# A backbone block on one core: a new order of the jobs of its first part, and five tiles of the second modulation's columns summed by TensorE instead of two

## The chip, the cores and the metric

The kernel is written in Tile for one NeuronCore of a Trainium2 chip. TensorE (PE in the profile), VectorE (DVE), ScalarE (ACT), GpSimd (POOL) and SyncE (SP, which only issues transfers here) each run their own instructions in order and wait for one another by semaphores. The metric is the device time of one execution in microseconds (us); lower is better. Three timed runs of the kernel before are given, and one profiled execution with its trace.

## The reference, cut to what matters

The block has one layer: a pooling mixer, a residual with layer norm, a SwiGLU feed-forward and a second residual with layer norm, over 1024 tokens of width 1024. A conditioning vector `c` gives six modulation vectors.

```python
mod_x = silu(c) @ mod_w + mod_b                   # (1024) @ (1024, 6144)
sh1, sc1, g1, sh2, sc2, g2 = split(mod_x, 6)
hx = x * (1.0 + sc1) + sh1
# window means (2, 4, 8, 16 tokens; one per 256 columns) less the row itself, then a 256x256 product per group
ox = multiscale_pool(hx, pool_w, pool_scale)
x = layer_norm(ALPHA * x + g1 * ox, ln_g[0], ln_b[0])
h = x * (1.0 + sc2) + sh2
gt, up = split(h @ ffn_w_in, 2)                   # 1024 -> 2 x 2816
x = layer_norm(ALPHA * x + g2 * ((silu(gt) * up) @ ffn_w_out), ln_g[1], ln_b[1])
```

All of it is in float32; the large products are made of three products of rounded parts (hi*hi, hi*lo, lo*hi), for which each operand is first split in two.

## The kernel before

It has three parts. The **first part** (to 227 us) computes everything up to the normalised rows and starts the feed-forward's gate products; the **loop** over 22 blocks of 128 hidden columns (to about 480 us) does the feed-forward's first product by a Strassen-like scheme; the **last part** does its second product, the residual and the last norm.

The first part is not written in the order in which it runs. Each step is a function, and `job` (L278) files it under its name and a running number, as mod_add.16. `carry_out` (L284) then calls the jobs in the order of the list `ORDER_OF_ISSUE` (L43). Each engine runs the instructions of its own jobs in just that order, so the list sets five queues at once. Which of the 45 large SBUF buffers, 8 PSUM banks and small rows a tile lies in is also a list, `PLACE_OF` (L111): a line is one place, its names are the tiles that use it one after another, and a tile waits until the one before it has been read.

The rows of x are worked on in two halves of four tiles of 128 tokens, `ORDER[0]` (rows 1 to 4) and `ORDER[1]` (5, 6, 7, 0). The jobs:

- mod_load (SP, L369) loads one 128x1024 tile of mod_w, 512 KB. Eight tiles make one modulation vector: mod_load.0 to .7 are SC1, .8 to .15 G1, .16 to .23 SC2, .24 to .31 SH2, .32 to .39 SH1.
- mod_add (DVE, L493, L491) adds a tile times its column of silu(c) into an accumulator. mod_col (PE, L513, L506) then sums the accumulator over the partitions into a column layout: eight matmuls of 128x128 by 128x64, 16 records in the trace. mod_whole (PE, L509, L506) does both for one tile straight from mod_w: again eight such matmuls, added up in the bank. `mod_columns(j, by_tensor)` (L523) makes mod_whole for the tiles in `by_tensor` and mod_add for the others. I call one mod_col or mod_whole a column pass. Before, SC2 had no tile by TensorE and SH2 had tiles 0 and 1 (`BY_TENSOR`, L35).
- pool_inner, pool_outer (PE, L457, L463) make the window means of 128 columns of a half in a bank, pool_hi (ACT) and pool_lo (DVE, L473) split them. Numbers 0 to 7 of pool_outer, pool_hi and pool_lo are the first half, 8 to 15 the second; pool_inner has four for each.
- scale_bank, g1_bank (PE) spread pool_scale and G1 over the partitions, make_g1 multiplies them, pool_w_weigh, pool_w_hi and pool_w_lo fold them and 1+SC1 into pool_w.
- pooled (PE, L587) is 12 matmuls for one row tile and one half of the columns: .0 to .7 are the first half's rows, .8 to .15 the second's. residual (DVE, L604) adds the row, mean, spread, factor and norm make the layer norm, keep_row stores it.
- mod_col_done, finish_gain and finish_shift (DVE) turn the column sums into per-partition factors. turned (PE, L691) transposes 128 columns of four rows, scaled_h (ACT) applies gain and shift, hidden_hi and hidden_lo split.
- gate_load, gate_hi, gate_lo prepare a pair's gate weights; gate_step (PE, L754) is six matmuls of 512 columns; there are 88. gate_first and gate_done (ACT) empty the banks, gate_out stores. Each step needs only the first half's rows.
- SH1's columns (mod_col.3), shift_through, shift_bank, shift_row and bend (among gate steps) correct two rows of the second half; turned.8 to .15 come after these rows' norms. difference, t_hi and t_lo make the loop's operands of them. weights_load, all_sums (POOL, L959), one_hi, two_hi, one_lo, two_lo prepare the loop's weights; `period` (L1233) is one turn of the loop.

The order of the loads on SP holds the stream of transfers: SC1 and rows, G1, pool_w, second rows, SC2, SH2, then gate weights.

Of the kernel before, what the change touches and what calls it, by code (L numbers as in the profile page):

```python
# [48 lines left out]
mod_load.11 mod_add.4 mod_load.12 mod_load.13 mod_load.14 pool_inner.11 pool_inner.3 mod_load.15 pool_inner.15
pool_inner.7 load_pool_w.0 load_pool_w.1 mod_add.5 load_x.4 pool_outer.2 load_x.5 pool_outer.0 pool_hi.2 pool_outer.3  # L50
pool_outer.1 load_x.6 pool_hi.0 pool_inner.24 pool_lo.2 pool_inner.16 load_x.7 pool_inner.25 pool_hi.3 pool_inner.17
mod_load.16 mod_add.6 pool_inner.28 pool_hi.1 pool_inner.20 mod_load.17 pool_inner.26 pool_inner.18 pool_inner.29
mod_load.18 pool_lo.0 pool_inner.21 start_band.0 scale_bank.0 mod_add.7 mod_load.19 end_band.0 scale_bank.1
scale_row.0 mod_add.8 mod_load.20 mod_col.0 scale_row.1 mod_add.9 mod_load.21 pool_inner.27 pool_outer.6
mod_col_done.0 pool_lo.3 pool_inner.19 pool_outer.4 pool_hi.6 pool_inner.30 mod_add.10 mod_load.22 pool_hi.4
pool_inner.22 pool_inner.31 pool_outer.7 pool_inner.23 pool_outer.5 pool_hi.7 mod_add.11 mod_load.23 pool_hi.5
mod_add.12 mod_load.24 mod_add.13 mod_load.25 mod_add.14 mod_load.26 mod_add.15 mod_load.27 g1_bank.0 pool_lo.1
pool_lo.6 pool_lo.4 g1_bank.1 pool_lo.7 pool_lo.5 make_g1.0 make_g1.1 pool_inner.40 pool_inner.32 pool_w_weigh.0
pool_inner.44 pool_w_weigh.1 pool_inner.36 pool_inner.41 pool_w_weigh.2 pool_inner.33 pool_w_weigh.3 pool_inner.56
pool_inner.48 pool_w_weigh.4 pool_inner.45 pool_w_hi.0 pool_inner.37 pool_w_weigh.5 pool_inner.42 pool_w_weigh.6  # L60
pool_inner.34 pool_inner.57 pool_w_lo.0 pool_inner.49 pool_inner.46 pool_inner.38 pool_inner.43 pool_outer.10 pooled.0
pool_w_weigh.7 pool_hi.10 mod_add.16 mod_load.28 pool_w_hi.1 pooled.2 residual.0 mod_add.17 mod_load.29 pooled.4
mod_add.18 mod_load.30 pool_inner.35 pool_outer.8 pool_inner.47 pool_hi.8 pool_outer.11 residual.2 pool_inner.39
pool_outer.9 pool_hi.11 pool_inner.59 mod_add.19 mod_load.31 gate_load.0 gate_load.1 gate_load.2 gate_load.3
gate_load.4 gate_load.5 pooled.6 pool_hi.9 mod_add.20 pool_outer.14 pool_inner.51 pool_outer.12 pool_inner.58
mod_add.21 pool_inner.50 pool_hi.14 pool_hi.12 residual.4 residual.6 pool_inner.60 mod_add.22 pool_inner.61
pool_inner.52 pool_inner.53 mod_add.23 pool_inner.63 pool_outer.15 pool_inner.55 pool_w_lo.1 pool_outer.13
pool_inner.62 pool_inner.54 pool_lo.10 pool_hi.15 mod_add.24 pool_hi.13 mod_whole.0 pool_lo.8 mod_add.25 mod_whole.1
mod_add.26 pooled.1 mod_add.27 residual.1 pooled.3 mod_add.28 mod_add.29 residual.3 mod_col.2 gate_hi.0 mean.0
spread.0 mean.1 gate_lo.0 pooled.5 spread.1 pool_lo.11 pooled.7 factor.0 residual.5 factor.1 norm.0 mod_col.1 mean.2  # L70
residual.7 keep_row.0 spread.2 mean.3 pool_lo.9 spread.3 pool_lo.14 pooled.12 factor.2 finish_gain.0 finish_shift.0
pooled.14 factor.3 norm.1 pool_lo.12 keep_row.1 norm.2 pool_lo.15 pooled.8 norm.3 pool_lo.13 keep_row.2 pooled.13
residual.12 keep_row.3 gate_hi.2 residual.14 turned.0 gate_hi.1 turned.1 residual.13 gate_lo.2 turned.2 scaled_h.0
turned.3 turned.4 scaled_h.1 gate_lo.1 turned.5 hidden_hi.0 turned.6 turned.7 pooled.15 residual.8 scaled_h.2
scaled_h.3 hidden_lo.0 hidden_hi.1 pooled.10 residual.15 scaled_h.4 hidden_lo.1 gate_step.0 scaled_h.5 hidden_hi.2
gate_step.1 residual.10 scaled_h.6 hidden_lo.2 scaled_h.7 gate_step.2 hidden_hi.3 gate_step.3 gate_hi.4 hidden_lo.3
gate_hi.3 gate_step.4 gate_lo.4 gate_hi.5 gate_lo.3 gate_step.5 gate_lo.5 gate_step.6 mod_load.32 gate_first.0
gate_step.7 mod_load.36 mod_add.30 gate_out.0 gate_first.1 gate_step.8 mod_load.33 gate_out.1 gate_step.9 mod_load.34
gate_step.10 mod_load.35 gate_step.11 gate_load.6 gate_load.7 gate_step.12 mod_add.31 gate_done.0 gate_out.2
gate_step.13 gate_step.14 mod_add.32 gate_step.15 load_pool_w.2 load_pool_w.3 mod_add.33 gate_first.2 gate_step.16  # L80
mod_load.37 mod_add.34 gate_out.3 gate_hi.6 gate_step.17 mod_load.38 gate_lo.6 gate_hi.7 gate_step.18 mod_load.39
gate_lo.7 gate_step.19 gate_load.8 gate_load.9 gate_step.20 gate_done.1 gate_out.4 gate_step.21 gate_step.22
mod_add.35 gate_step.23 gate_first.3 gate_step.24 gate_out.5 gate_step.25 mod_add.36 gate_step.26 mod_add.37
gate_step.27 gate_load.10 gate_load.11 gate_hi.8 gate_lo.8 mod_col.3 gate_done.2 gate_out.6 gate_hi.9 gate_step.28
mod_col_done.1 shift_through.0 gate_step.29 gate_lo.9 gate_step.30 shift_through.1 gate_hi.10 gate_step.31 gate_lo.10
gate_first.4 gate_step.32 gate_out.7 gate_hi.11 gate_step.33 gate_lo.11 gate_step.34 gate_step.35 gate_load.12
gate_load.13 gate_step.36 gate_done.3 gate_out.8 gate_hi.12 gate_step.37 gate_lo.12 gate_step.38 gate_hi.13
gate_step.39 gate_lo.13 gate_first.5 gate_step.40 gate_out.9 gate_step.41 gate_step.42 gate_step.43 gate_load.14
gate_load.15 gate_step.44 gate_done.4 gate_out.10 gate_hi.14 gate_step.45 gate_lo.14 gate_step.46 gate_hi.15
gate_step.47 weights_load.0 gate_lo.15 gate_first.6 gate_step.48 gate_out.11 gate_step.49 gate_step.50 gate_step.51  # L90
gate_load.16 gate_load.17 all_sums.0 gate_step.52 gate_done.5 gate_out.12 gate_step.53 one_hi.0 one_lo.0 gate_hi.16
gate_step.54 gate_lo.16 gate_step.55 two_hi.0 gate_first.7 shift_bank.0 two_lo.0 gate_out.13 gate_hi.17 gate_step.56
shift_row.0 gate_lo.17 shift_bank.1 pooled.9 bend.0 bend.2 pooled.11 residual.9 gate_step.57 residual.11 gate_step.58
shift_row.1 bend.1 bend.3 gate_step.59 gate_load.18 gate_load.19 gate_hi.18 gate_hi.19 gate_lo.18 gate_step.60
gate_done.6 gate_lo.19 gate_out.14 gate_step.61 mean.6 spread.6 gate_step.62 mean.7 mean.4 mean.5 spread.7 factor.6
gate_step.63 p1_load.0 weights_load.1 gate_first.8 gate_step.64 factor.7 gate_out.15 spread.4 gate_step.65 spread.5
gate_step.66 factor.4 gate_step.67 gate_load.20 gate_load.21 factor.5 norm.6 keep_row.6 norm.7 gate_step.68 keep_row.7
norm.4 gate_step.69 keep_row.4 norm.5 gate_step.70 keep_row.5 gate_done.7 gate_step.71 gate_out.16 gate_hi.20
gate_lo.20 gate_first.9 gate_step.72 gate_out.17 gate_hi.21 gate_step.73 gate_lo.21 gate_step.74 turned.8 turned.10
scaled_h.8 gate_step.75 scaled_h.10 gate_done.8 turned.12 turned.14 gate_out.18 scaled_h.12 turned.9 scaled_h.14  # L100
turned.11 turned.13 scaled_h.9 turned.15 scaled_h.11 difference.0 gate_step.76 scaled_h.13 scaled_h.15 difference.4
gate_step.77 hidden_hi.4 difference.1 gate_step.78 hidden_hi.5 difference.5 t_hi.0 gate_step.79 gate_first.10 t_lo.0
# [1302 lines left out]
```

## Time and profile before

| what | value |
|---|---|
| time of the three runs, median (lowest to highest) | 761.9 us (760.66 to 762.62) |
| the profiled execution's own time | 765.08 us |
| its span, first to last instruction | 763.3 us |
| mean granted TensorE clock | 0.962 |
| busy share of the span: PE, DVE, ACT, POOL | 96%, 73%, 36%, 22% |
| first gate product, first product of the loop (starts) | 97.7 us, 227.4 us |

A busy share is an average over parts with different limits, so the stretches are to be read one by one. The granted clock is a share of TensorE's full clock; it is 1.00 (2.4 GHz) or 0.50 (1.2 GHz) at any moment. Matmuls overlap, so that the time from one start to the next is shorter than the duration of one. The share of DMA is that of the core's 16 transfer engines.

### The profile page before, as it was taken

Reading aid. Unit: us, or ns where it says so; the run is one execution under the profiler, and the core shown is the slowest. Engines: PE = TensorE matmul, PEld = TensorE weight load, DVE = VectorE, ACT = ScalarE, POOL = GpSimd, SP = SyncE. Lnnn points to the kernel's source line nnn. Section 1 sums busy time; section 2 is a strip of 40 time slices with the busy share of each in tenths; the row PEclk is TensorE's granted clock in tenths of the full one; section 3 lists DMA queues with packets and bytes.
Section 4 is the critical chain, followed back from the end, with each engine's and each line's share of the span. In section 5 each row is a group of like instructions: output and inputs, shape, how many; then the busy total and the mean of one; then the engine's idle time right before and its main releaser. Section 6 shows DMA issues by size and latency. Waiting matters only on the chain.

```text
span 763.3 us, 9102 instructions
## 1 busy us (share of the span) xinstructions
PE 730.3 (96%) x3326; PEld 605.9 (79%) x3326; DVE 559.9 (73%) x675; ACT 275.0 (36%) x353; POOL 165.6 (22%) x126
## 2 busy tenths in 40 slices
PE   6988999999999999999999999999879999999995
PEld 5767988888887888888888888888558888888784
DVE  3598855517198797988889979865369689747985
ACT  0212873435982312213122131123247634344311
POOL 0000000020207554734736447421000000000000
PEclk7578999999999999999999999999999999999998
DMA  8998249685838689999998999699999975764412
GB/s 297 344 409 301 112 148 378 219 247 165 304 113 285 209 276 298 265 278 250 282 297 287 295 202 259 214 288 275 303 365 389 340 234 191 232 229 152 164 58 83
DMA packets 117731, 191.51 MB, mean 251 GB/s; under 512 B 7627, under 2 KB 66707, under 8 KB 117174
## 3 DMA queue, kind: packets, MB, share of 16 engines
...
HBM read 150.79 MB, written 66.06 MB: 284 GB/s over the span
## 4 chain that ended last, share of the span: by engine, by line
PE 65%; issue 16%; DMA 11%; DVE 5%; ACT 2%; POOL 0%; SPq 0%; POOLq 0%; DVEq 0%; ACTq 0%
PE ps_v L895 33%; PE ps_gate L761 13%; PE ps_x L1103 7%; DMA yraw<-in_ffn_w_out 4%; PE ps_y L1103 4%; DMA line_lb<-in_ln_b 3%; PE ps_col L506 2%; DVE acc L491 2%; PE ps_pt L461 1%; DMA a11d<-a 1%; PE ps_ox L262 1%; PE ps_ox L264 1%; PE ps_ox L263 1%; DMA x<-in_x 1%; DVE t L270 1%
## 5 line engine op out<-in xcount | busy, mean ns | idle before, releaser
L270 DVE TENSOR_TENSOR ylo<-yraw,yhi 128x1024 fp32r<-128x1024 f32 x77 | 91.8, 1221 | 34.4 <-ACT yhi L267 23.6
L267 ACT CAST yhi<-yraw 128x1024 fp32r<-128x1024 f32 x77 | 80.0, 1052 | 94.4 <-PE ps_x L1103 31.7
L895 PE MATMUL ps_v<-t,w0h 128*128 128x512 f32 x352 | 109.2, 392 | 0.0
L761 PE MATMUL ps_gate<-h,wih 128*128 128x512 f32 x352 | 109.0, 391 | 0.0
L962 POOL TENSOR_TENSOR s<-raw,raw 128x512 f32<-128x512 f32 x22 | 33.1, 1504 | 320.4 <-DMA raw<-in_ffn_w_in 312.0
L918 ACT ACTIVATE a<-a 128x512 f32<-128x512 f32 x22 | 13.9, 632 | 230.0 <-DVE a L917 230.0
L895 PEld LDWEIGHTS ps_v<-t,w0h 128*128 128x128 f32 x352 | 66.1, 188 | 14.5 <-issue 1.0
L761 PEld LDWEIGHTS ps_gate<-h,wih 128*128 128x128 f32 x352 | 65.7, 188 | 13.8 <-issue 0.5
L1103 PE MATMUL ps_x<-yhi 128*128 128x512 f32 x176 | 69.6, 395 | 5.1 <-ACT u L1310 2.7
L1103 PE MATMUL ps_x<-ylo,yhi 128*128 128x512 f32 x176 | 69.8, 397 | 3.3 <-DVE ylo L270 3.3
L491 DVE SCALAR_TENSOR_TENSOR acc<-mw,s_col,acc 128x1024 f32<-128x1024 f32 x42 | 54.9, 1307 | 23.1 <-DMA mw<-in_mod_w 22.5
L895 PE MATMUL ps_v<-t,w0l 128*128 128x512 f32 x176 | 68.6, 390 | 1.5 <-DVE w0l L270 1.5
L1103 PE MATMUL ps_x<-yhi,ylo 128*128 128x512 f32 x176 | 69.2, 393 | 0.0
L761 PE MATMUL ps_gate<-h,wil 128*128 128x512 f32 x176 | 68.5, 389 | 0.0
L895 PE MATMUL ps_v<-t,ws 128*128 128x512 f32 x264 | 63.4, 389 | 0.0
L895 PEld LDWEIGHTS ps_v<-t,ws 128*128 128x128 f32 x264 | 49.5, 188 | 10.3
L895 PE MATMUL ps_v<-t,w1h 128*128 128x512 f32 x176 | 54.1, 389 | 0.0
L895 PE MATMUL ps_v<-h,w1h 128*128 128x512 f32 x176 | 54.1, 389 | 0.0
L1103 PE MATMUL ps_y<-yhi 128*128 128x512 f32 x132 | 51.4, 390 | 0.9 <-DVE yv L1348 0.9
L1103 PE MATMUL ps_y<-ylo,yhi 128*128 128x512 f32 x132 | 51.4, 389 | 0.0
L1103 PE MATMUL ps_y<-yhi,ylo 128*128 128x512 f32 x132 | 51.3, 389 | 0.0
L1125 POOL TENSOR_TENSOR yrow<-yrow,line_lg 128x224 f32<-128x224 f32 x1 | 0.9, 913 | 229.3 <-ACT yrow L1185 229.3
...
## 6 DMA issues: line engine op xcount, KB each, us to landing
...
```

The lines of the kernel that those rows point to most:

```text
L262: nc.tensor.matmul(ps, lh, rh, start=first, stop=False)
L263: nc.tensor.matmul(ps, lh, rl, start=False, stop=False)
L264: nc.tensor.matmul(ps, ll, rh, start=False, stop=last)
L267: nc.scalar.copy(hi, src)
L270: nc.vector.tensor_tensor(lo, src, hi.bitcast(F32), ALU.subtract)
L491: nc.vector.scalar_tensor_tensor(acc, w, s_col[:, k : k + 1], acc, ALU.mult, ALU.add)
L506: nc.tensor.matmul(tiles["ps_col", j][:, n * WIDE : (n + 1) * WIDE], t[:, n * P : (n + 1) * P], by, start=first and n == 0, stop=last and ...
L761: nc.tensor.matmul(ps, x, y, start=k == n == 0, stop=k % 4 == 3 and n == 2, skip_group_check=k > 3)
L895: nc.tensor.matmul(ps, x, y, start=fresh and first, stop=last, skip_group_check=not fresh)
L918: nc.scalar.activation(a[:, 1], a[:, 1], ACT.Silu)
L962: nc.gpsimd.tensor_tensor(s, up1, up2, ALU.add)
L1103: nc.tensor.matmul(ps, s[x][:, r * P : (r + 1) * P], t[y][:, d], start=fresh and j == m == 0, stop=j == PAIRS - 1 and m == 2, skip_group_c ...
```

## The change

The list `ORDER_OF_ISSUE` is replaced by another order of the jobs, `PLACE_OF` by another plan of the places (with the same 45, 8 and 8 places), and two lines choose which tiles TensorE sums. The functions are the same. The diff without the two lists:

```diff
-BY_TENSOR = (0, 1)
+BY_TENSOR = (5, 6, 7)
...
-    mod_columns(SC2, ())
+    mod_columns(SC2, (6, 7))
     job(finish_gain)
     mod_columns(SH2, BY_TENSOR)
     job(finish_shift)
```

So SC2 has six mod_add (.16 to .21) and mod_whole.0 and .1; SH2 has five mod_add (.22 to .26) and mod_whole.2 to .4; SH1's are now .27 to .34. There are three mod_add fewer and three column passes more.

TensorE's jobs by the two lists, with the numbers of a repeated job put together (before, then after):

```text
before:
warm_up.0 to_columns.0 pool_inner.8,0,12,4 to_columns.1 pool_inner.9,1,13,5,10,2,14,6,11,3,15,7 pool_outer.2,0,3,1 pool_inner.24,16,25,17,28,20,26,18,29,21 scale_bank.0,1 mod_col.0 pool_inner.27 pool_outer.6 pool_inner.19 pool_outer.4 pool_inner.30,22,31 pool_outer.7 pool_inner.23 pool_outer.5 g1_bank.0,1 pool_inner.40,32,44,36,41,33,56,48,45,37,42,34,57,49,46,38,43 pool_outer.10 pooled.0,2,4 pool_inner.35 pool_outer.8 pool_inner.47 pool_outer.11 pool_inner.39 pool_outer.9 pool_inner.59 pooled.6 pool_outer.14 pool_inner.51 pool_outer.12 pool_inner.58,50,60,61,52,53,63 pool_outer.15 pool_inner.55 pool_outer.13 pool_inner.62,54 mod_whole.0,1 pooled.1,3 mod_col.2 pooled.5,7 mod_col.1 pooled.12,14,8,13 turned.0-7 pooled.15,10 gate_step.0-27 mod_col.3 gate_step.28-55 shift_bank.0 gate_step.56 shift_bank.1 pooled.9,11 gate_step.57-74 turned.8,10 gate_step.75 turned.12,14,9,11,13,15 gate_step.76-87

after:
warm_up.0 to_columns.0 pool_inner.0,4,12,8 to_columns.1 pool_inner.1,9,5,13,10,6,2,14,15,3,7,11 pool_outer.0,1,3,2 pool_inner.20,16,17,28 scale_bank.1,0 pool_inner.29-31 pool_outer.7 pool_inner.18,19 pool_outer.4 pool_inner.21-23 pool_outer.5 mod_col.0 pool_inner.24-27 pool_outer.6 g1_bank.0 pool_inner.40 g1_bank.1 pool_inner.56,44,45,32,35 pool_outer.8 pool_inner.59 pool_outer.14 pool_inner.47 pool_outer.11 pool_inner.33,34,36,39 pool_outer.9 pool_inner.37,41,42,57,58,52,43 pool_outer.10 pool_inner.38 pooled.4,0,1 pool_inner.55 pool_outer.13 pool_inner.53 pooled.6,5,7,2 pool_inner.46,54 pooled.3 mod_whole.0-4 mod_col.1,2 pooled.10,14 turned.0,1,4,7,5,6,2,3 pooled.8,12 pool_inner.60-63 pool_outer.15 pool_inner.48,51 pool_outer.12 pool_inner.49,50 gate_step.0-7 pooled.11,15,9,13 gate_step.8-24 mod_col.3 gate_step.25-27 shift_bank.0,1 gate_step.28-39 turned.10,11,15,9 gate_step.40 turned.13,12 gate_step.41,42 turned.8,14 gate_step.43-87
```

DVE's jobs from the sums of G1 to the columns of SH2 (before, then after):

```text
before:
mod_add.9 mod_col_done.0 pool_lo.3 mod_add.10-15 pool_lo.1,6,4,7,5 make_g1.0,1 pool_w_weigh.0-6 pool_w_lo.0
pool_w_weigh.7 mod_add.16 residual.0 mod_add.17,18 residual.2 mod_add.19-21 residual.4,6 mod_add.22,23 pool_w_lo.1
pool_lo.10 mod_add.24 pool_lo.8 mod_add.25-27 residual.1 mod_add.28,29 residual.3 mean.0,1 gate_lo.0 ...

after:
mod_add.9-13 pool_lo.4 mod_add.14,15 mod_col_done.0 pool_lo.5,2,3,6,7 make_g1.0 pool_w_weigh.1,3,0,2 make_g1.1
pool_w_weigh.6,5,7,4 pool_w_lo.0 mod_add.16 pool_w_lo.1 residual.4 mod_add.17 residual.0,1 mod_add.18 residual.6
mod_add.22 residual.5 mod_add.23 residual.7,2 mod_add.19 residual.3 mod_add.20 mean.1,0,3,2 mod_add.21,24,25
factor.1,3 mod_add.26 factor.0 pool_lo.10,14,8 finish_gain.0 pool_lo.9,11 finish_shift.0 factor.2 ...
```

Further in the new order: the second half's means, spreads, factors and norms stand earlier among the gate steps (norm.5 and .4 near gate_step.8, norm.7 and .6 before gate_step.40 instead of near gate_step.68); difference, t_hi and t_lo stand among gate_step.40 to .65 instead of from gate_step.75 to behind gate_step.87; pooled.11, .15, .9 and .13 stand behind gate_step.7. On SP the loads keep their order; the keep_row jobs move with their norms. In the plan of places the eight first pooled products have two banks in turn, which mod_whole.0 and mod_whole.2 take over from residual.2 and residual.3.

## Rows read from the trace of the kernel before

**Rows 1.** The busy time of each engine by stretch. The columns are the stretch in us from the span's start, its length, the busy time (and number of instructions) of PE, PE's weight loads, DVE, ACT and POOL, the granted clock, the share of the transfer engines, and GB/s.

```profile
20.80:40.20 19.40, 19.32 (x67) 15.44 (x67) 11.86 (x13) 6.23 (x13) 0.00 (x0) 0.50 1.00 355
40.20:43.66 3.46, 0.57 (x3) 0.49 (x3) 3.39 (x4) 0.59 (x1) 0.00 (x0) 0.50 1.02 407
43.66:49.20 5.54, 5.54 (x14) 3.46 (x15) 5.20 (x10) 0.00 (x0) 0.00 (x0) 0.50 1.03 410
49.20:65.65 16.45, 16.45 (x120) 14.95 (x119) 15.28 (x24) 5.52 (x9) 0.00 (x0) 1.00 1.03 400
65.65:67.33 1.68, 0.08 (x2) 0.00 (x1) 1.68 (x3) 0.96 (x2) 0.00 (x0) 1.00 1.09 348
67.33:69.68 2.35, 2.35 (x21) 2.35 (x22) 2.35 (x3) 1.05 (x1) 0.00 (x0) 1.00 1.09 349
69.68:75.00 5.32, 5.29 (x25) 4.99 (x24) 2.62 (x3) 0.00 (x0) 0.00 (x0) 0.50 0.62 198
75.00:75.76 0.76, 0.00 (x1) 0.01 (x1) 0.75 (x3) 0.00 (x0) 0.00 (x0) 0.50 0.00 0
75.76:79.92 4.16, 4.16 (x20) 4.16 (x20) 3.63 (x7) 0.34 (x1) 0.00 (x0) 0.50 0.00 0
79.92:97.60 17.68, 17.68 (x153) 17.68 (x153) 14.63 (x35) 17.43 (x25) 0.00 (x0) 1.00 0.38 141
97.60:227.40 129.80, 129.80 (x607) 108.06 (x606) 66.51 (x93) 78.25 (x108) 10.79 (x8) 1.00 0.66 225
227.40:240.44 13.04, 11.51 (x52) 9.20 (x50) 10.04 (x9) 6.46 (x9) 6.92 (x6) 1.00 0.82 249
240.44:480.00 239.56, 239.56 (x1053) 197.60 (x1054) 209.44 (x220) 51.77 (x68) 129.33 (x90) 1.00 0.93 269
480.00:763.30 283.30, 264.67 (x1147) 215.50 (x1145) 205.34 (x251) 104.91 (x119) 16.95 (x15) 0.99 0.72 234
```

**Rows 2.** DVE in order of time, 26 to 45 us: start, duration, line and operation, number of them, and in brackets the idle time before it and what ended it.

```profile
27.50 3.86 DVE L491 SCALAR_TENSOR_TENSOR acc<-mw,s_col,acc 128x1024 f32<-128x1024 f32 x3 [2.90 <-DMA mw<-in_mod_w]
34.95 0.17 DVE L518 SCALAR_TENSOR_TENSOR sc<-ps_col,cols 128x8 f32<-128x8 f32 x1 [3.59 <-PE ps_col L506]
...
35.63 7.88 DVE L491 SCALAR_TENSOR_TENSOR acc<-mw,s_col,acc 128x1024 f32<-128x1024 f32 x6
43.43 1.88 DVE L474 TENSOR_TENSOR pt<-ps_pt,pt 128x512 fp32r<-128x512 f32 x3
```

**Rows 3.** The list of waits of TensorE: who waited for whom, total us, times, longest.

```profile
PE ps_g L548 <- DVE acc L491: 2.9, 1, 2.9
...
PE ps_col L506 <- DVE pt L474: 1.6, 1, 1.6
PE ps_v L895 <- DVE w0l L270: 1.5, 1, 1.5
...
PE ps_ox L262 <- DVE x L608: 0.8, 1, 0.8
```

**Rows 4.** DVE in order of time, 62 to 80 us, columns as in rows 2.

```profile
68.45 3.92 DVE L491 SCALAR_TENSOR_TENSOR acc<-mw,s_col,acc 128x1024 f32<-128x1024 f32 x3
75.01 0.69 DVE L608 SCALAR_TENSOR_TENSOR x<-x,ps_ox 128x512 f32<-128x512 f32 x1 [2.64 <-PE ps_ox L264]
...
75.62 2.60 DVE L491 SCALAR_TENSOR_TENSOR acc<-mw,s_col,acc 128x1024 f32<-128x1024 f32 x2
```

**Rows 5.** TensorE alone by stretch (column passes, transposes, two pooled products): length, PE's busy time and records, granted clock, share of the transfer engines, GB/s.

```profile
69.68:72.06 2.38, 2.38 (x13) 0.50 1.06 337
78.48:80.87 2.39, 2.39 (x17) 0.70 0.02 7
83.82:85.53 1.71, 1.71 (x19) 1.00 0.00 0
91.37:94.78 3.41, 3.41 (x34) 1.00 0.76 300
94.78:97.73 2.95, 2.95 (x27) 1.00 0.49 137
```

**Rows 6.** Groups of instructions from 0 to 98 us: their number, total busy us, mean ns of one, and idle time before them.

```profile
L491 DVE SCALAR_TENSOR_TENSOR acc<-mw,s_col,acc 128x1024 f32<-128x1024 f32 x27 | 34.6, 1284 | 10.9 <-DMA mw<-in_mod_w 10.4
...
L629 ACT ACTIVATE sq<-x,mv 128x1024 f32<-128x1024 f32 x4 | 4.6, 1138 | 10.6 <-DVE mv L624 10.6
...
L630 ACT ACT_TABLE_LOAD x1 | 1.3, 1283 | 0.1
```

**Rows 7.** POOL, ACT and DVE in order of time at the start of the loop, columns as in rows 2. The rows of three answers stand one below the other.

```profile
233.06 1.28 POOL L962 TENSOR_TENSOR s<-raw,raw 128x512 f32<-128x512 f32 x1 [32.40 <-DMA raw<-in_ffn_w_in]
...
234.37 0.62 ACT L267 CAST ws<-s 128x512 fp32r<-128x512 f32 x1 [3.15 <-POOL s L962]
234.90 1.05 ACT L267 CAST t<-h 128x1024 fp32r<-128x1024 f32 x1
...
235.98 2.18 DVE L270 TENSOR_TENSOR t<-h,t 128x1024 fp32r<-128x1024 f32 x1 [3.00 <-ACT t L267]
238.08 2.30 DVE L270 TENSOR_TENSOR w0l<-raw,w0h 128x1024 fp32r<-128x1024 f32 x1
```

**Rows 8.** One idle stretch of TensorE in the last part, columns as in rows 1.

```profile
570.30:573.04 2.74, 0.00 (x0) 0.00 (x1) 2.74 (x3) 2.46 (x4) 0.00 (x0) 1.00 1.03 401
```

**Rows 9.** ACT in order of time: the split of the first gate tile, columns as in rows 2.

```profile
67.89 1.05 ACT L267 CAST wih<-wi 128x1024 fp32r<-128x1024 f32 x1 [1.27 <-DMA wi<-in_ffn_w_in]
```

More of the change, by code (lines that the diff above doesn't have):

```diff
@@ L49 @@
[L49 to L102, printed above, removed]
-gate_step.80 gate_out.19 t_hi.4 hidden_lo.4 gate_step.81 difference.2 t_hi.1 gate_step.82 t_hi.5 difference.3 t_hi.2
@@ new lines @@
+gate_load.4 gate_load.5 mod_whole.0 residual.3 mod_add.20 mod_whole.1 mean.1 mean.0 mean.3 spread.1 mean.2 mod_add.21
+mod_whole.2 mod_add.24 mod_whole.3 spread.3 mod_add.25 factor.1 spread.0 mod_whole.4 factor.3 mod_add.26 norm.1
+factor.0 mod_col.1 pool_lo.10 norm.3 keep_row.1 pool_lo.14 pool_lo.8 norm.0 keep_row.3 mod_col.2 finish_gain.0
+spread.2 pool_lo.9 keep_row.0 pool_lo.11 pooled.10 finish_shift.0 gate_hi.0 factor.2 pooled.14 norm.2 residual.10
+gate_lo.0 turned.0 gate_hi.2 keep_row.2 turned.1 turned.4 residual.14 scaled_h.0 turned.7 gate_lo.2 scaled_h.4
@@ new lines @@
+gate_lo.1 gate_step.6 mod_load.32 mod_add.27 gate_first.0 gate_step.7 mod_load.36 pool_lo.13 gate_out.0 gate_first.1
+pooled.11 gate_out.1 pooled.15 residual.11 mean.5 spread.5 pooled.9 residual.15 pooled.13 factor.5 residual.9 norm.5
+mean.4 gate_step.8 mod_load.33 residual.13 spread.4 keep_row.5 mod_add.28 gate_step.9 mod_load.34 factor.4 norm.4
+gate_step.10 mod_load.35 keep_row.4 gate_step.11 gate_load.6 gate_load.7 gate_done.0 mod_add.29 gate_step.12
+mod_add.30 gate_step.13 gate_out.2 mod_add.31 gate_step.14 gate_hi.6 gate_step.15 load_pool_w.2 load_pool_w.3
@@ new lines @@
+gate_step.28 gate_lo.11 gate_step.29 bend.2 gate_step.30 bend.0 shift_row.1 gate_step.31 bend.1 gate_first.4 mean.6
+gate_step.32 bend.3 spread.6 gate_out.7 mean.7 gate_step.33 gate_step.34 spread.7 factor.6 gate_step.35 gate_load.12
+gate_load.13 gate_done.3 factor.7 gate_step.36 gate_step.37 norm.7 gate_out.8 gate_step.38 gate_hi.12 keep_row.7
+gate_step.39 norm.6 gate_lo.12 gate_first.5 turned.10 keep_row.6 turned.11 turned.15 scaled_h.10 gate_out.9 turned.9
+scaled_h.11 gate_step.40 gate_hi.13 difference.4 turned.13 turned.12 gate_lo.13 t_hi.4 gate_step.41 scaled_h.12 t_lo.4
```

164 lines of the change are left out of this document (102 added, 62 removed).

## The prediction

> **What bounds the kernel now.** I read the busy time by stretch first [rows 1]. From 97.60 us to the end of the first part at 227.40 TensorE is busy in every microsecond at a granted clock of 1.00, and from 240.44 to 480 in 239.56 of 239.56. The last stretch has gaps, but none of its code changes. So everything between 97.6 and 480 is as long as TensorE's work is, and the first part can be shortened in three ways only: less idle time of TensorE ahead of 97.6, less work at the half clock (0.50, the 1.2 GHz level) there, or less TensorE work. The reader is to see four places in [rows 1]: 40.20 to 43.66 (busy 0.57 of 3.46), 65.65 to 67.33 (0.08 of 1.68), 75.00 to 75.76 (nothing), and the clock at 0.50 from 69.68 to 79.92. One place more lies behind the first part: 227.40 to 240.44, busy 11.51 of 13.04. The lists of waits say whom TensorE waited for there: DVE in each case [rows 3].
>
> The sum goes against the profiled span, 763.3 us; that execution took 765.08, 3.2 above the median of the three timed runs, 761.9 (760.66 to 762.62). I carry the difference over to the median as it is. A change under 0.3% (2.3 us) can't be told from none here.
>
> **1. The wait for g1_bank: -3.2 us.** Before, DVE stands behind mod_col_done.0: its third sum ends at 31.36, it idles 3.59 us for the column sums on PE, and only then adds the last six G1 tiles, from 35.63 to 43.51 [rows 2]. g1_bank.0 waits 2.9 us for that [rows 3]. The new order puts mod_add.10 to .15 ahead of mod_col_done.0, with two pool_lo among them. From 27.50: nine sums at 1.31 (7.88 over six) and two pool_lo at 0.6 give 40.5 instead of 43.51. The tiles are there: at 407 to 410 GB/s [rows 1] one of 0.524 MB takes 1.28 us, so the eighth after 27.50 lands near 37.8. PE has its other work of this stretch done at 39.8 to 40.2, as before. g1_bank.0 then starts at 40.5, not 43.66.
>
> **2. The two later gaps: -2.4 us.** They end with DVE releases [rows 3, 4]: DVE does sums and residuals in turn, 1.3 us [rows 6] and 0.6 us [rows 4], and is behind from 45 to 79 us. Two things help it: three sums of 1.3 us leave it (-3.9 us of DVE work, of no worth by itself, since DVE then waits for PE), and its sums of SC2 and SH2 are put between the residuals. I walked it from the start of the first pooled product (call it S, near 52.6: g1_bank 3.2 earlier, about 3 us more pool work ahead of it). With 1.47 us for a pooled product [rows 5], two banks in turn, and on DVE residual, sum, residual, residual, sum and so on, residual.2 ends at S+11.6, residual.3 at S+13.6, mod_add.21 at S+17.0 and mod_add.26 at S+21.6. PE reaches mod_whole.0 at S+12.8 (needs residual.2), mod_whole.2 at S+16.3 (residual.3), mod_col.1 at S+21.4 (mod_add.21), mod_col.2 at S+23.2 (mod_add.26). None waits, the closest by 1.2 us. The last tile of SH2 has landed: the first gate tile, loaded behind it, ends a wait at 67.89 [rows 9], and mod_whole.4 comes at S+19, 71.6.
>
> **3. The half clock from 69.68 to 79.92: -4.2 us.** The clock fell 2.35 us into mod_whole, which followed 1.68 us of idle time [rows 1]. At the half clock 13 records of a column pass took 2.38 us, at the full clock 107 ns each (1.71 for 16): 1.0 us lost [rows 5]. Two pooled products took 2.72 each (75.76 to 78.48) for 1.47: 2.5. The next pass took 2.39 for 1.71: 0.7. In the new order the passes follow eight pooled products without a gap. I take the loss as gone; rival A is that it isn't. The rise at 49.20 [rows 1] should come about 3 us earlier, as the g1_bank products do.
>
> The Trainium skill's TensorE: Matmul & The Clock Gate (section Why this matters for your kernels) puts a fall of the clock down to idle gaps between matmuls; by it seven gapless passes stay at 2.4 GHz and this sum stands. The same page (Part 4: PE-mode transpose) says that transposes don't count as activity in the same way, which speaks against the change: 32 of them follow the passes, and by that rule rival A, with its time, would be the likelier. In this trace 32 transposes, between pooled products, kept 1.00.
>
> That last row is 91.37 to 94.78 [rows 5]; also 2.74 us of plain idle at 570.30 left the clock at 1.00 [rows 8]. So a short stretch of thin work alone need not cost it; what fell had idle time and thin work together.
>
> **4. Three passes more: +5.1 us.** Each mod_whole is 16 matmul records and weight loads; 1.71 us at the full clock, 2.93 at the half (13 records in 2.38) [rows 5]. They are TensorE work ahead of a saturated stretch, so nothing hides them. Lower end 5.1, upper end 8.8.
>
> **5. Work moved past the start of the gate products: 0.** Two pooled products (12 instead of 14 ahead of it) and the last window sums go among or close to the gate steps. By the walk gate_step.0 starts at S+38.5, about 91, not 97.6, and what follows is 129.8+2.9. TensorE is saturated and at full clock there; moving costs nothing unless it brings a wait.
>
> **6. New waits: +1.8 us (0 to 5).** No row of before shows them; each is the end of a chain by the durations of [rows 2, 4 to 6] and a gate step's 1.36 us (129.80 less the other work, by 88). pooled.10 needs pool_lo.11, which now stands behind finish_gain: S+25.6 against S+24.9, 0.7 us. pooled.11 needs pool_lo.13, behind four weight splits and mod_add.27, whose tile is loaded only when pooled.12 has freed its place: 0.3. shift_bank.1 stands three gate steps behind mod_col.3 and needs eight DVE operations in between: none to 0.9. turned.10 needs norm.6, which on ACT stands behind spread.6, spread.7, gate_done.3 and two table loads: 0.7. Their sum is 1.7 to 2.6; I take 1.8. The ends: nothing, if each is 1 us earlier than I have it, and 5 if each is 1 us later. On PE all gate steps queue behind such a wait. SP and POOL: SP's loads keep their order, four keep_row and the gate_out move with their producers; POOL has nothing until all_sums.
>
> **7. The wait in the second period of the loop: -1.5 us.** Before, TensorE waited 1.5 us for w0l [rows 3]. The chain is in [rows 7]: raw tiles land at 233.06, ACT's ws waits for POOL's sum, and behind it in ACT's queue stands the last t_hi (234.90); DVE waits for it (idle 3.00), then does t_lo, and only then w0l, which ends at 240.4. In the new order all t_hi and t_lo are done by gate_step.65, so w0l no longer stands behind them.
>
> **Sum**: -3.2 -2.4 -4.2 +5.1 +1.8 -1.5 = -4.4, hence 761.9 - 4.3 = 757.6.
>
> **Rivals.**
> A, slower: the clock falls within the seven passes (five mod_whole, two mod_col, 12 us of the same thin matmuls), at mod_whole.0 or behind it. For it: the fall at 69.68 came inside such passes. Against: that had 1.68 us of idle time ahead. It decides if idle time of about a microsecond comes next to the passes, so at mod_whole.0 (1.2 us of room) or at pooled.10 (0.7 us of wait forecast). Price, from a fall as far into them as in before (21 records): 5.7 passes by 2.93-1.71 = 7.0, two pooled 2.5, transposes at the same ratio 2.4, less about 1 for the waits of step 6 that it covers: +10.9, so 768. A fall only behind them costs 2 to 4 and lands at 760 to 761.
> B, no difference: the waits of step 6 come out at 5 us or over, because the chains on DVE and ACT are dense (from 79.92 to 97.60 ACT is busy 17.43 of 17.68 [rows 1], and that density now begins while PE does the passes). -4.4+3.2 gives 760.7.
> C, no difference: the clock doesn't rise with g1_bank but only with the pooled products, some 7 us of window sums at half clock; these lose about 3 us. 760.6.
> D, better: no new wait and a still earlier rise: 755.5.
>
> **How the numbers follow.** Forecast 0.52 (755.5 to 759.6), D 0.10, B 0.18, C 0.08, A 0.12. Faster by over 0.3% (under 759.6): forecast and D and a fifth of B and C, 0.67. Within 0.3%: the rest of B and C, 0.21. Slower: A, 0.12. The range leaves out most of A and the lower half of D: 754.8 to 763.6. That takes in 5 us of new waits and the half-clock price of the passes up to its 3.7 us above the lower end.
>
> **What would show it.** g1_bank at 40.5 and pooled.4 near 52.6 (steps 1, 5); five mod_whole near 65.5 with no idle time ahead and the clock at 1.00 until the gate steps (2, 3); first gate product near 91; gaps of under 1 us at pooled.10, pooled.11, shift_bank and turned.10 (6); first loop product 2 to 3 us before 227.4, and no wait for w0l in the second period (7). Wrong would be: 0.50 in the passes, a gap of over 2 us in the gate products, or a first gate product later than 94.

## The result, and the profile after

The changed kernel took 756.88 us (median of 10 executions, 755.04 to 759.77) beside 760.89 for the kernel before (10 executions): ratio 0.9943, 95% interval 0.9919 to 0.9966, by the ratio 4.3 us less (2.6 to 6.2). Timed once more it was 756.05 beside 761.39, 0.9934 (0.9914 to 0.9955). 757.6 was forecast. The profiled execution took 758.19 us, its span is 756.4.

The busy time by stretch of the changed kernel, columns as in [rows 1]. The stretches begin with g1_bank (40.41), the fall of the clock (48.46), the first pooled product (55.59), the first column pass (68.58), pooled.10 (81.00), the first gate product (93.12), the loop (225.82) and the last part (526.82).

```profile
40.41:48.46 8.05, 5.91 (x26) 3.64 (x25) 7.98 (x16) 2.12 (x3) 0.00 (x0) 0.92 1.03 409
48.46:55.59 7.13, 7.13 (x30) 6.58 (x31) 1.97 (x3) 2.25 (x4) 0.00 (x0) 0.52 1.03 409
55.59:68.58 12.99, 12.99 (x109) 12.84 (x109) 9.94 (x19) 1.53 (x3) 0.00 (x0) 1.00 1.04 385
68.58:81.00 12.42, 12.42 (x114) 12.42 (x113) 11.55 (x26) 10.02 (x15) 0.00 (x0) 1.00 0.57 197
81.00:93.12 12.12, 12.12 (x103) 11.82 (x102) 8.71 (x16) 11.82 (x17) 0.00 (x0) 1.00 0.37 129
93.12:225.82 132.70, 132.70 (x632) 110.76 (x630) 78.36 (x101) 79.12 (x109) 16.85 (x10) 1.00 0.67 227
225.82:240.44 14.62, 14.62 (x66) 12.12 (x65) 9.09 (x9) 4.07 (x6) 6.03 (x4) 1.00 0.70 243
...
526.82:756.40 229.58, 213.83 (x925) 173.98 (x923) 168.73 (x207) 93.69 (x105) 1.66 (x2) 0.98 0.68 231
```

From 55.59 to the end of the loop TensorE has no idle time and the clock is 1.00: the passes keep the full clock, the gate products wait for nothing, and the wait for w0l at the loop's start is gone. What had not been foreseen is in the first two rows: 2.14 us of idle time, and then 7.1 us at 0.52. The list of TensorE's waits, columns as in [rows 3], says whom it waited for. None of the four waits of [rows 3] is left, but the x tiles, in the list of before with 5.9 us, now cost 9.8:

```profile
PE ps_pt L461 <- DMA x<-in_x: 9.8, 6, 4.7
PE ps_x L1103 <- DVE ylo L270: 2.9, 4, 0.8
PE ps_x L1103 <- ACT u L1310: 1.6, 1, 1.6
PE ps_x L1103 <- ACT yhi L267: 1.4, 2, 1.2
PE ps_warm L321 <- DVE ones L311: 1.1, 1, 1.1
PE ps_y L1103 <- DVE yv L1348: 0.9, 1, 0.9
```

TensorE in order of time shows two of these waits ahead of the fall, and the passes and transposes at the full clock:

```profile
42.74 0.46 PE L461 MATMUL ps_pt<-consts,x 128*128 128x130 f32 x2 [0.62 <-DMA x<-in_x]
...
46.48 0.49 PE L461 MATMUL ps_pt<-starts,x 128*128 128x128 f32 x2 [1.53 <-DMA x<-in_x]
...
68.58 9.04 PE L506 MATMUL ps_col<-s_col,mw 128*128 128x64 f32 x80
77.46 3.74 PE L506 MATMUL ps_col<-ones,acc 128*128 128x64 f32 x32
83.96 3.65 PE L694 MATMUL ps_h<-ident,x 128*128 128x128 f32 x32
```

One execution is not enough here: the starts below differ by 3 us between executions of the same code. So all profiles stand in one table, in us, read as the start of the first g1_bank, pooled, gate and loop product and of the first product of the last part (ps_x). "To gate" is from the first pooled product to the first gate product, and so on; the last part is the span less the start of ps_x. The groups E1 to E4, E5 to E8 and E9 to E12 ran on one chip each, three chips in all.

| kernel | g1_bank | pooled | to gate | to loop | loop | last part | span |
|---|---|---|---|---|---|---|---|
| before, first profile | 43.7 | 52.4 | 45.3 | 129.7 | 302.9 | 233.0 | 763.3 |
| E9: before again | 40.5 | 48.0 | 47.5 | 129.7 | 302.9 | 232.1 | 760.1 |
| E8: before, raw tile early | 40.9 | 49.6 | 45.3 | 129.7 | 302.2 | 231.9 | 758.8 |
| E5: before, no idle time | 40.1 | 49.1 | 42.3 | 129.7 | 302.6 | 232.3 | 756.0 |
| after, first profile | 40.4 | 55.6 | 37.5 | 132.7 | 301.0 | 229.6 | 756.4 |
| E10: after again | 41.0 | 54.1 | 37.5 | 132.7 | 301.0 | 232.0 | 757.3 |
| E4: after, raw tile late | 40.7 | 52.6 | 37.5 | 135.0 | 301.0 | 229.3 | 755.4 |
| E3: after, two sums moved | 40.9 | 52.9 | 38.7 | 132.9 | 301.0 | 229.4 | 755.0 |
| E7: after, three sums moved | 39.5 | 50.9 | 52.9 | 132.7 | 301.0 | 231.6 | 769.1 |
| E6: after, two passes back | 40.0 | 50.4 | 41.5 | 133.1 | 301.0 | 232.0 | 758.0 |
| E12: after, G1 sums late | 41.2 | 52.9 | 37.5 | 134.0 | 301.0 | 232.1 | 757.5 |
| E1: after, x tiles first | 41.6 | 51.9 | 37.5 | 133.4 | 301.0 | 229.8 | 753.6 |
| E2: after, last x tile late | 41.1 | 51.9 | 38.7 | 132.7 | 301.0 | 229.3 | 753.6 |
| E11: E1 with one pass less | 41.2 | 51.9 | 37.0 | 133.0 | 301.0 | 230.4 | 753.3 |

The pair taken on one chip, E9 and E10, gives the ledger: +6.10 to the first pooled product, -9.95 from there to the first gate product, +3.02 to the loop, -1.87 in the loop, -0.09 behind it, together -2.79, the difference of the spans. It is the ledger of this pair and not of the medians: E10's profiled execution, at 759.09 us, was the longest of its six, and the +6.1 holds a fall of the clock that E3, E4, E6 and E7 don't have.

The first two profiles seemed to show 3.4 us in the last part, whose code is unchanged. E9 and E10 agree there within 0.1, but not at the same clock: E10 is at 0.50 for 6.8 us in it (550.8 to 557.6), E9 for 3.4. E11, on their chip and with 3.4 us at 0.50, took 230.4. So what the change gives there stays open. Only 0.4 us of it is steady: from the last instruction of VectorE, ScalarE and POOL to the end of the span it is 3.14 to 3.15 us in all four profiles of the old order and 2.73 to 2.74 in all ten of the new one.

### The profile page after: what moved, and what is told of

Same layout as the page of the kernel before. It is cut to its first block, busy times and chain, and to the rows that moved or that the text cites. A ratio compares the mean times of both kernels' runs of the same rounds, so it can differ in the third digit from the quotient of the medians.

```text
span 756.4 us, 9186 instructions
## 1 busy us (share of the span) xinstructions
PE 729.8 (96%) x3374; PEld 607.1 (80%) x3374; DVE 551.2 (73%) x672; ACT 275.0 (36%) x353; POOL 169.0 (22%) x126
## 4 chain that ended last, share of the span: by engine, by line
PE 71%; issue 14%; DMA 12%; SPq 1%; DVE 1%; ACT 0%; POOL 0%; POOLq 0%
PE ps_v L895 35%; PE ps_gate L761 16%; PE ps_x L1103 8%; PE ps_y L1103 4%; DMA yraw<-in_ffn_w_out 3%; DMA mw<-in_mod_w 3%; DMA line_lb<-in_ln_b 2%; PE ps_col L506 2%; DMA x<-in_x 1%; PE ps_pt L461 1%; DMA a11d<-a 1%; PE ps_ox L262 1%; PE ps_ox L264 1%; PE ps_ox L263 1%; PE ps_h L694 1%
## 5 line engine op out<-in xcount | busy, mean ns | idle before, releaser
L761 PEld LDWEIGHTS ps_gate<-h,wih 128*128 128x128 f32 x352 | 65.6, 188 | 13.7 <-ACT wih L267 0.2
L491 DVE SCALAR_TENSOR_TENSOR acc<-mw,s_col,acc 128x1024 f32<-128x1024 f32 x39 | 52.0, 1334 | 18.7 <-DMA mw<-in_mod_w 18.3
## 6 DMA issues: line engine op xcount, KB each, us to landing
mw<-in_mod_w SPq DMA_DIRECT2D x48, 512.0 KB, 10.2
```

Of the source, the lines that this page charges most:

```text
L491: nc.vector.scalar_tensor_tensor(acc, w, s_col[:, k : k + 1], acc, ALU.mult, ALU.add)
L761: nc.tensor.matmul(ps, x, y, start=k == n == 0, stop=k % 4 == 3 and n == 2, skip_group_check=k > 3)
```

## The experiments

Diffs of the order of jobs show the jobs that move and their neighbours.

**E9 and E10, both kernels again.**

> The kernel before once more, unchanged, for the spread of one execution. In its first profile the first pooled product is at 52.4, the first loop product at 227.4, the loop takes 302.9 us and the last part 233.0. Two kernels with the same first part (the two experiments on the kernel before) had the first pooled product at 49.1 and 49.6. If those are the usual, the first profile was a late execution: first pooled product near 49.5, g1_bank near 40.5, first loop product near 224.5 here. Otherwise 52.4, 43.7 and 227.4.

> The changed kernel once more, unchanged. In its first profile the clock fell at 48.7 and the first pooled product was at 55.6; four experiments with the same code up to there had it at 50.4 to 52.9 and no fall. If the fall was of that execution: first pooled product 50.5 to 53, first loop product 222 to 224, time 756 to 757 at the median. If it belongs to the kernel: 55 to 56 and 225.8 again. The last part, run on the same chip as the kernel before of this set, tells whether its 229.6 against 233.0 us is of the change: if so, this run is 3 us shorter there than the other; if not, the two agree within 1.

g1_bank came at 40.5 and the first pooled product at 48.0: the first profile of before was a late execution, as E5 and E8 say too. E9 is one execution, of 761.86 us. E10 has the fall of the clock once more, though E3, E4, E6 and E7, the same code up to there, have none. The wait for the last x tile ahead of it tells them apart: 1.53 us in the first profile and 1.52 in E10, 0.44 to 0.53 in E4, E6 and E7, none in E3. TensorE in order of time, E10 and then E4:

```profile
46.57 0.49 PE L461 MATMUL ps_pt<-starts,x 128*128 128x128 f32 x2 [1.52 <-DMA x<-in_x]
```

```profile
46.62 0.49 PE L461 MATMUL ps_pt<-starts,x 128*128 128x128 f32 x2 [0.49 <-DMA x<-in_x]
```

VectorE in order of time in E9, columns as in [rows 2]:

```profile
25.71 1.28 DVE L491 SCALAR_TENSOR_TENSOR acc<-mw,s_col,acc 128x1024 f32<-128x1024 f32 x1 [0.86 <-DMA mw<-in_mod_w]
27.55 2.60 DVE L491 SCALAR_TENSOR_TENSOR acc<-mw,s_col,acc 128x1024 f32<-128x1024 f32 x2 [0.55 <-DMA mw<-in_mod_w]
31.84 0.17 DVE L518 SCALAR_TENSOR_TENSOR sc<-ps_col,cols 128x8 f32<-128x8 f32 x1 [1.69 <-PE ps_col L506]
...
32.53 7.88 DVE L491 SCALAR_TENSOR_TENSOR acc<-mw,s_col,acc 128x1024 f32<-128x1024 f32 x6
```

and in E10:

```profile
26.69 1.28 DVE L491 SCALAR_TENSOR_TENSOR acc<-mw,s_col,acc 128x1024 f32<-128x1024 f32 x1 [2.42 <-DMA mw<-in_mod_w]
...
30.77 6.57 DVE L491 SCALAR_TENSOR_TENSOR acc<-mw,s_col,acc 128x1024 f32<-128x1024 f32 x5 [0.75 <-DMA mw<-in_mod_w]
...
37.85 2.60 DVE L491 SCALAR_TENSOR_TENSOR acc<-mw,s_col,acc 128x1024 f32<-128x1024 f32 x2
```

The idle time that step 1 counts on is 1.69 us in E9 and was 3.59 in [rows 2]. In E10 it is gone, but the nine sums begin 1.0 us later, behind a tile that lands late, and have two pool_lo among them: they end at 40.45 as against 40.41.

**E12, the G1 sums late again.**

```diff
-scale_row.1 pool_lo.1
+scale_row.1 mod_col.0 pool_lo.1
...
-pool_outer.7 mod_add.10
+pool_outer.7 mod_col_done.0 mod_add.10
...
-pool_outer.5 mod_col.0 pool_hi.5
+pool_outer.5 pool_hi.5
...
-pool_inner.27 mod_col_done.0 pool_outer.6
+pool_inner.27 pool_outer.6
```

> The changed kernel with the column sums of SC1 on TensorE and mod_col_done.0 on VectorE put ahead of the last six G1 sums again, as before; nothing behind them is moved. Step 1 of the prediction: g1_bank comes 3.2 us later, at 43.7, and so does the first pooled product. Theory from the experiments on the kernel before, where g1_bank came at 40.1 and 40.9: the 3.59 us of idle time in the first profile were longer than usual there because the G1 tiles came late in that execution; g1_bank comes 0.5 to 1.5 us later than in the changed kernel run beside it.

One execution, 759.26 us: g1_bank at 41.2, 0.2 us later than in E10, the first pooled product at 52.9. The order that step 1 priced at 3.2 us is worth nothing measurable at g1_bank.

**E1 and E2, the x tiles.** E1 moves their loads, E2 eight window sums that don't need the last tile.

```diff
-load_pool_w.0 pool_inner.11 mod_add.5 load_pool_w.1 load_x.4
+load_x.4 load_x.5 load_x.6 load_x.7 load_pool_w.0 pool_inner.11 mod_add.5 load_pool_w.1
```

```diff
-pool_inner.32 pool_inner.35
+pool_inner.32 pool_inner.33 pool_inner.34 pool_inner.36 pool_inner.37 pool_inner.41 pool_inner.42 pool_inner.57 pool_inner.58 pool_inner.35
```

> The changed kernel with the four loads of the second half's x tiles issued ahead of the two pool weight tiles instead of behind them; nothing else differs. Theory 1: the late landing of these tiles is what put the first pooled product at 55.6 us instead of the 52.6 forecast. TensorE waited 0.62 us (at 42.74) and 1.53 us (at 46.48) for them, and the granted clock fell to 0.50 from about 48.7 to 55.1 because of that idle time. With the tiles 2.6 us earlier both waits go (-2.2 us) and the fall with them (about -3 us): first pooled product 50.5 to 52.5, the later end set by the pool weights, which now land last; time 752 to 754. Theory 2: the fall comes from the thin window sums themselves, idle or not. Then only the waits go, the first pooled product is at 53.4, time about 754.7. Rival: the pool weights, some 5 us later, take the place of the x tiles, the first pooled product stays at 55 or later, and the time is that of the changed kernel, 757, or worse.

> The changed kernel with eight window sums that need no last x tile put ahead of the six that need it or follow it (tile columns 0 to 2 of the second half ahead of column 3); the loads stay as they are. Theory 1 (idle time made the clock fall): the 1.53 us wait for the last tile at 46.48 goes, 0.6 us at 42.74 stays, and the half clock from 48.7 to 55.1 goes with the longer wait: first pooled product 51.5 to 53, time 753 to 755. Theory 2 (thin work made it fall): only 1.5 us are gained, first pooled product at 54, time 755.4, and 0.50 is still seen for some 6 us.

755.61 us (0.9908, 0.9874 to 0.9941) and 755.59 (0.9906, 0.9877 to 0.9936): both waits are gone in both, the first pooled product is at 51.9. Both medians are above what their first theories gave, 752 to 754 and 753 to 755. In E1 the clock rises at 44.6 and then stays at 1.00 through the first part and the loop. In E2 it fell without any idle time, as its busy time by stretch shows (columns as in [rows 1]):

```profile
48.00:50.00 2.00, 2.00 (x12) 1.59 (x12) 2.00 (x4) 1.75 (x3) 0.00 (x0) 1.00 1.01 397
50.00:52.00 2.00, 2.00 (x12) 1.78 (x11) 1.16 (x2) 0.73 (x2) 0.00 (x0) 0.79 1.04 414
52.00:54.00 2.00, 2.00 (x12) 2.00 (x11) 0.00 (x0) 0.71 (x2) 0.00 (x0) 0.50 1.02 406
```

So idle time is not the only thing behind a fall among the window sums; these are thin too (thin: matmuls of few columns). That fall costs 1.2 us (38.7 for 37.5). The intervals of E1 and E2 overlap with that of the changed kernel: neither is shown to be better.

**E3 and E7, idle time put ahead of the passes.** E3 moves two sums, E7 mod_add.21 as well.

```diff
-pool_inner.54 residual.2 pooled.3
+pool_inner.54 mod_add.19 mod_add.20 residual.2 pooled.3
```

> The changed kernel with two of VectorE's sums moved ahead of residual.2, whose bank the first of the seven column passes writes: TensorE should idle some 2.2 us ahead of the passes, as it idled 1.68 us ahead of the two passes before. Theory 1 (idle time next to thin passes makes the clock fall, as rival A of the prediction has it): the clock falls to 0.50 some 2 us into the passes; with 2.2 us of idle time, 1.2 us more for each pass at the half clock and 2.4 for the two pooled products and the transposes, the first gate product is 6 to 14 us later than 93.1 and the time is 763 to 771. Theory 2 (the passes keep 1.00 whatever stands ahead, and the fall of before had another cause): only the 2.2 us, time 759.

> The changed kernel with three of VectorE's sums ahead of residual.2 where the earlier experiment had two, which gave 0.96 us of idle time ahead of the seven passes and no fall of the clock. One sum more is 1.3 us, so about 2.2 us of idle time, more than the 1.68 that came before the fall in the kernel before. Theory 1 (idle time of that size next to thin passes makes the clock fall): 0.50 within or behind the passes, the first gate product 6 to 14 us later than in the changed kernel, time 763 to 771. Theory 2: the clock stays at 1.00, only the 2.2 us are lost, time 759.

E3 idled 0.96 us, not 2.2, and the clock held in its profile. Seven of its ten executions took 756.75 to 760.58 us (their ratio is 0.9943, 0.9919 to 0.9966), the other three 769.8 to 773.1 at a mean clock of 0.954 to 0.956. E7 idled 2.28 us and took 770.4 and 770.9 us (1.0113, 1.0083 to 1.0142) at 0.954. TensorE in order of time, E7:

```profile
66.33 16.70 PE L506 MATMUL ps_col<-s_col,mw 128*128 128x64 f32 x80 [2.28 <-DVE x L608]
82.82 7.04 PE L506 MATMUL ps_col<-ones,acc 128*128 128x64 f32 x32
94.67 3.65 PE L694 MATMUL ps_h<-ident,x 128*128 128x128 f32 x32
```

and its stretches, columns as in [rows 1]:

```profile
66.00:68.00 2.00, 1.67 (x11) 1.67 (x12) 1.96 (x9) 0.83 (x1) 0.00 (x0) 0.76 1.09 348
...
76.00:94.00 18.00, 18.00 (x85) 18.00 (x86) 3.52 (x12) 4.92 (x7) 0.00 (x0) 0.50 0.24 95
94.00:96.00 2.00, 2.00 (x19) 2.00 (x18) 1.53 (x3) 0.70 (x1) 0.00 (x0) 0.91 0.00 0
```

The first five passes take 16.70 us where the changed kernel needs 9.04, and the clock is back only at 94.4. This is rival A: 52.9 us instead of 37.5 to the first gate product. An idle time of 2.3 us, made by VectorE's order alone, costs over 13. That E3's three long executions had the same fall is likely by their clock; they were not profiled.

**E5, the idle time of before taken away.**

```diff
-mod_add.23 pool_inner.63
+pool_lo.10 mod_add.23 pool_inner.63
...
-pool_inner.54 pool_lo.10 pool_hi.15
+pool_inner.54 pool_hi.15
```

> The kernel before with one VectorE job moved: pool_lo.10, for which the first column pass waited 1.60 us, stands two jobs of 1.3 and 1.2 us earlier. Its two passes stay as they are. Theory 1 (idle time next to thin passes makes the clock fall): the 1.68 us of idle time ahead of the passes go, the clock stays at 1.00 and the 4.2 us lost at the half clock from 69.68 to 79.92 are not lost: the first loop product comes 5 to 6.5 us before 227.4 unless ScalarE's chain ahead of the gate products takes its place, time 755 to 757. Theory 2 (the thin passes make it fall by themselves): 0.50 is still seen behind the passes, only 1.7 us are gained, time 760. It also shows once more how long the unchanged last part takes, from the loop's last product to the end: 233.0 us in the profile before, 229.6 after; if that difference is of the execution and not of the change, it is about 229.5 here.

758.05 us (0.9944, 0.9924 to 0.9965): one job moved by two places gives the kernel before as much as the whole change. TensorE in order of time, E5:

```profile
62.24 3.68 PE L506 MATMUL ps_col<-s_col,mw 128*128 128x64 f32 x32
69.58 0.39 PE L262 MATMUL ps_ox<-wpsh,pt 128*128 128x256 f32 x1 [2.18 <-DVE x L608]
```

The two passes have no wait ahead of them and run in 3.68 us, as at the full clock; in E9 they took 6.68. But a wait of 2.18 us for a residual is there now, five us behind the start of the passes, and after it the clock is at 0.50 from 70.0 to 73.4 in place of 63.9 to 77.5 in E9.

**E6, SC2's two passes back on VectorE.**

```diff
-    mod_columns(SC2, (6, 7))
+    mod_columns(SC2, ())
```

with the two sums right behind mod_add.21 in the order.

> The changed kernel with the two last tiles of the fifth modulation's columns (SC2) summed by VectorE again, right behind mod_add.21; the three of SH2 stay on TensorE. The step of the prediction (a pass is 1.71 us of TensorE that nothing hides): 3.4 us less, time 753.5. Rival: VectorE's two sums more, 2.6 us, make mod_col.1 wait 1.2 us and mod_col.2 some 2.7, and the 3.4 us come back as idle time, time 757; if that idle time also makes the clock fall, 761 or more.

762.48 us (0.9996, 0.9979 to 1.0013): by the ratios, 0.0053 and 0.0062 above the changed kernel's two, 4.0 to 4.7 us more, though TensorE has 3.4 us less to do. TensorE in order of time, E6:

```profile
64.31 5.57 PE L506 MATMUL ps_col<-s_col,mw 128*128 128x64 f32 x48 [0.79 <-DVE x L608]
69.82 2.00 PE L506 MATMUL ps_col<-ones,acc 128*128 128x64 f32 x16
74.07 3.68 PE L506 MATMUL ps_col<-ones,acc 128*128 128x64 f32 x16 [2.25 <-DVE acc L491]
```

The rival: mod_col.2 waits 2.25 us for VectorE's last sum, the clock falls there (0.50 from 72.5 to 82.7), and the pass behind it takes 3.68 for 2.00.

**E11, one pass less with room for its sum.** As E1, with SC2 at `(7,)` and VectorE's SC2 sums one place earlier:

```diff
-residual.4 mod_add.17 mod_load.29 pooled.1
+mod_add.17 mod_load.29 residual.4 mod_add.18 mod_load.30 pooled.1
```

> The changed kernel with the x tiles loaded ahead of the pool weights, as in the first experiment (755.6), with one of SC2's two passes given back to VectorE, and with each of VectorE's SC2 sums moved one place ahead, into the idle time of 1.4 to 4.4 us that it has before the first residual. A pass is 1.71 us of TensorE; VectorE's later work is as long as it was. Theory (a pass costs its 1.71 us wherever VectorE has room for its sum): no new wait of TensorE over 0.5 us, six passes, first gate product 1.7 us earlier for the same start of the pooled products, 753.9. Rival: pooled.10 and mod_col.2 now come up before pool_lo.11 and mod_add.27 and wait for what is saved, so 755 to 756; or this idle time makes the clock fall, 760.

755.78 us (0.9930, 0.9914 to 0.9946), no better than E1. The pass is saved, and 1.05 us of it come back as a wait further on (TensorE in order of time, E11):

```profile
79.94 3.50 PE L694 MATMUL ps_h<-ident,x 128*128 128x128 f32 x30 [1.05 <-ACT x L645]
```

The transposes now come up before ScalarE's norm, a wait that neither theory named.

**E4 and E8, the wait at the loop's start.** Both change one line, in the changed kernel (place 33) and in the kernel before (place 40):

```diff
-        free[kind] = deque(n for n in range(count) if n not in used)
+        free[kind] = deque(sorted((n for n in range(count) if n not in used), key=lambda n: (kind, n) != ("big", 33)))
```

> The changed kernel with the loop's list of free places begun with the place that the last gate product frees (about 225.8), so that the first raw weight tile of the loop's third period is loaded at about 225.9 instead of 215.13; in the kernel before it was issued at 225.63. The order of t_hi and t_lo stays as changed. Theory of the prediction (w0l was late because it stood behind the last t_hi and t_lo on ScalarE and VectorE): no wait for w0l in the second period, first product of the third period as in the changed kernel. Rival: w0l was late because its raw tile was loaded late; then the wait for w0l in the second period is back, 1.5 us or more (3 if it only follows from the 1.6 us by which TensorE is earlier there).

> The kernel before with the loop's list of free places begun with the place that gate_out.20 frees, so that the first raw tile of the third period is loaded at about 220 instead of 225.63; t_hi and t_lo stay late. If w0l was late because the last t_hi stood behind ws on ScalarE, and ws behind this load, then ws is 5 us earlier, t_hi and t_lo with it, and the wait for w0l in the second period, 1.5 us, goes without any change of order. If the wait stays, the late t jobs themselves are enough. The last part, whose code is unchanged, took 233.0 us in the profile before and 229.3 to 229.8 in the changed kernel and the experiments on it; about 229.5 here would say that the 233.0 belong to that execution.

Each is one execution, 757.29 us (E4) and 760.55 (E8). In E4 the raw tile was issued at 225.32, and POOL's sum on it began at 233.66 (POOL in order of time), as late as in [rows 7], yet TensorE has no idle time there (columns as in [rows 1]):

```profile
233.66 1.40 POOL L962 TENSOR_TENSOR s<-raw,raw 128x512 f32<-128x512 f32 x1 [26.10 <-DMA raw<-in_ffn_w_in]
```

```profile
225.00:245.00 20.00, 20.00 (x90) 16.57 (x89) 12.57 (x13) 5.99 (x8) 10.94 (x8) 1.00 0.96 293
```

So the late load does nothing once the t jobs are out of the way: the rival falls. In E8 the load came at 217.3 and the wait shrank from 1.5 to 0.3 us: the chain of [rows 7], load, sum, ws, last t_hi, w0l, can be cut at either end. The 135.0 us of E4 in the table hold 1.9 us of TensorE waiting at turned.10 for a norm, the wait that step 6 priced at 0.7.

## Why the prediction was right, and where it was not

The total was right to 0.7 us by luck: two terms that were wrong had opposite signs.

**Step 1 failed.** It took the 2.9 us wait for g1_bank as time that the new order gives back. The wait is in every profile of before, but g1_bank comes at 40.1 to 40.9 there in three of four, and at 39.5 to 41.6 in the changed kernel and what was made of it: no gain. The 43.66 of the profile was one late execution. The 3.2 us that it stood above the median were not to be carried over as they were: E9, close to the median, has a span 3.2 us shorter, with g1_bank 3.1 and the first pooled product 4.4 us earlier. What the step counts in passing, 3 us more of window sums ahead of the pooled products, is then a plain loss. 52.6 was forecast for the first pooled product; it came at 50.4 to 52.9 in E3, E4, E6 and E7, and at 54.1 and 55.6 in the two profiles of the changed kernel itself, but before it had been at 48.0 to 49.6, not 52.4. The step also looked only at the modulation tiles; the x tiles' landing and the half clock behind the wait for the last of them are the rest (rival C had such a half clock, for another reason). E9 and E12, one profile each, show the first part, E1 the second; E2 shows that the wait isn't the only way to that fall.

**Steps 2 and 3 were right in mechanism and too small.** -6.6 forecast; with the passes, and with no wait of step 6 ahead of the gate products, the way from the first pooled to the first gate product was to be 38.5 us, 6.8 less than before. It is 37.5, and 7.8 to 10.0 less, since the half clock of before lasts 13.7 us in E9 (63.9 to 77.5) for 10.2 in the first profile. That the passes' idle time brings the fall is shown from both sides: taken away in E5, put in in E7. In all fourteen profiles, behind the first g1_bank and ahead of the first gate product, each of the eight idle times of 1.52 to 2.28 us was followed by a fall; those of 0.44 to 1.05 us alone were not.

Where the prediction went wrong here is its reading of [rows 8]: "what fell had idle time and thin work together". In the same trace, 12 us ahead of that stretch, idle times of 2.04 and 0.76 us among products of 512 columns were followed by 0.50 from 557.78 to 561.19. E9 has the same behind 3.20 us (TensorE in order of time, then the busy time by stretch, columns as in [rows 1]):

```profile
568.22 0.51 PE L1103 MATMUL ps_x<-yhi 128*128 128x512 f32 x1 [3.20 <-ACT u L1310]
```

```profile
569.06:572.48 3.42, 3.42 (x10) 2.66 (x9) 3.42 (x4) 3.06 (x5) 0.00 (x0) 0.50 1.06 392
```

So thin work isn't needed for a fall, and how long the idle time was doesn't decide it alone: 2.74 us brought none.

The Trainium skill's TensorE: Matmul & The Clock Gate (Why this matters for your kernels) has falls come from idle gaps between matmuls. Ahead of the column passes the runs agree, though their gaps are shorter than those that the page warns of: 1.60 us in E9 and 2.28 in E7 brought one, no idle time in the changed kernel brought none; E2's fall, with no gap, the rule doesn't explain. By the same page (Part 4: PE-mode transpose) transposes don't count as activity in the same way; here 32 of them, behind seven passes and two pooled products, 83.96 to 87.61, stayed at 1.00.

**Step 4 was right as a size, wrong as a cost by itself.** Five passes in 8.88 us (68.58 to 77.46) are 1.78 each for 1.71. But E6 shows what the 5.1 us bought: with two passes fewer the kernel is 4 to 5 us slower.

**Step 5 was right**: +3.0 behind the start of the gate products for 2.9 forecast. **Step 6** (1.8, bounds 0 to 5) came out at 0 in both profiles of the changed kernel; E4's 1.9 at turned.10 shows that it is a matter of a few us of slack. **Step 7 was right**, -1.9 for -1.5, by the chain that it named (E4). Rival A is real (E7) but didn't occur; B and D didn't occur.

In numbers, forecast against E9 and E10: first pooled product +0.2 against +6.1, to the gate products -6.8 against -10.0, to the loop +4.7 (2.9 and 1.8) against +3.0, loop -1.5 against -1.9. The walk thus summed to -3.4, a little under the -4.4 of the terms, and -4.4 from 761.9 is 757.5, not 757.6.

Open: why the tile that VectorE waits for at 26.7 lands later in the new order, why the last x tile is waited for 1.5 us in two profiles of the changed code and 0.53 or less in the others, what tips the clock in E2, and what the last part owes to the change.
